# Multiply and GELU on one core: the last y load in shrinking pieces, the stores in growing ones

## Chip, core, metric

The kernel runs on one core of one Trainium2 chip. The metric is the device time of one execution in microseconds, as the median of several runs. All runs told of here were in the fast state, and the granted clock was 1.00 in each. The rounds of the experiments ran on different chips, so each run is compared with the kernel before in its own rounds.

## The reference

```python
x, y: float32, 1024 x 4096
z = x * y
out = 0.5 * z * (1 + tanh(sqrt(2 / pi) * (z + 0.044715 * z ** 3)))   # float32
```

16.8 MB are read for x, 16.8 MB for y, and 16.8 MB are written: 50.33 MB for two operations per element.

## The kernel before

Each tensor is viewed as 128 rows of 32768 columns, one row per SBUF partition (128 KB a row). x stays in SBUF whole and is overwritten in place; y passes through a ring of 16384 columns. All transfers are issued by SyncE (SP) into one queue. VectorE multiplies 4096 columns at a time, ScalarE applies GELU to them, and two stores of 16384 columns close the kernel.

```python
X_LOADS = [(0, 16384), (16384, 32768)]
Y_LOADS = [(0, 16384, 0), (16384, 24576, 0), (24576, 32768, 8192)]   # from, to, place in the ring
STEP = 4096
STORES = [(0, 16384), (16384, 32768)]
# ...
    _hoist(nc, [load_x(0).ins, load_y(0).ins])      # issued ahead of the start barrier
    load_x(1)
    for i in (1, 2):                                # a ring place is free after its multiplication
        nc.sync.wait_ge(sem_mul, (Y_LOADS[i][1] - Y_LOADS[1][0]) // STEP)
        load_y(i)
    n = 0
    for i, (a, b, r) in enumerate(Y_LOADS):
        # ... VectorE waits for x and y ...
        for c in range(a, b, STEP):
            nc.vector.tensor_mul(out=xs[:, c : c + STEP], in0=xs[:, c : c + STEP],
                in1=ys[:, r + c - a : r + c - a + STEP]).then_inc(sem_mul, 1)
            n += 1
            nc.scalar.wait_ge(sem_mul, n)
            nc.scalar.activation(out=xs[:, c : c + STEP], in_=xs[:, c : c + STEP],
                func=GELU).then_inc(sem_act, 1)
    for i, (a, b) in enumerate(STORES):
        nc.sync.wait_ge(sem_act, b // STEP)
        nc.sync.dma_start(out=out_r[:, a:b], in_=xs[:, a:b]).then_inc(sem_o[i], 16)
# ... wait for the stores, clear the semaphores ...
```

## Time and profile before

| | before |
|---|---|
| time, median of the 3 runs known at the prediction | 121.03 us (120.79 to 121.08) |
| span of the profiled run | 119.5 us |
| VectorE busy, ScalarE busy | 35.0 us, 30.2 us |
| share of the DMA queue's packets in 16 engines' span | 98.5% |
| last store issued; its first packets | 93.3 us; 99.3 us |

Some readings rest on the packet records of the trace, which lie under the profile's DMA rows. Each record is one packet of one engine with start, duration and size. A partition row is one packet here (896 data packets for 7 transfers of 128 rows), and after each transfer comes a packet of 4 bytes per engine (112 of them), followed by the 16 increments of its semaphore. I also use the times at which these 16 semaphore increments land, as the mean over the engines. In the rows of digits, the GB/s rows and the stretches below, a packet's time and bytes are counted whole where it starts.

### The profile page before, as it was taken

The page shows a single profiled execution, that of the slowest core. Times are in us where ns is not written, and L with a number is a line of the kernel's source. Part 1 is how long each engine was busy: PE and PEld are TensorE (multiplying, and loading weights), DVE is VectorE, ACT ScalarE, POOL GpSimd, SP SyncE. Part 2 cuts the span into 40 slices and gives each one's busy share as a digit, 9 for nine tenths or more (in the row PEclk, how much of TensorE's full clock was granted, in tenths as well). Part 3 has the DMA queues.
Part 4 walks back from the last instruction along what each step waited for, and adds up shares of the span by engine and source line. Part 5 has one row for each costly group of instructions (what it writes and reads, how often), then busy time and mean ns, then how long its engine had stood idle before and what let it go on. Part 6 is the DMA issues. An engine that isn't in the chain of part 4 may idle for free.

```text
span 119.5 us, 68 instructions
## 1 busy us (share of the span) xinstructions
DVE 35.0 (29%) x8; ACT 30.2 (25%) x9; POOL 0.2 (0%) x4
## 2 busy tenths in 40 slices
DVE  0000000000000199999600049959990000000000
ACT  3000000000000006797780000977479200000000
POOL 0000000000000000000000000000000000000000
DMA  9889888998899889988898989998899888988890
GB/s 351 351 373 680 351 351 351 636 417 351 351 636 417 351 351 526 526 351 351 351 526 351 504 373 482 395 526 351 351 395 658 351 351 351 702 351 351 351 680 22
DMA packets 1008, 50.33 MB, mean 421 GB/s; under 512 B 112, under 2 KB 112, under 8 KB 112
## 3 DMA queue, kind: packets, MB, share of 16 engines
q1 hardware_dynamic: 1008, 50.33, 98.5%
HBM read 33.55 MB, written 16.78 MB: 421 GB/s over the span
## 4 chain that ended last, share of the span: by engine, by line
DMA 53%; DVE 22%; ACT 3%; SPq 0%; issue 0%; DVEq 0%
DMA ys<-in_y_dram 53%; DVE xs L87 22%; ACT xs L94 3%; SPq L66 0%; DVEq L85 0%
## 5 line engine op out<-in xcount | busy, mean ns | idle before, releaser
L87 DVE TENSOR_TENSOR xs<-xs,ys 128x4096 f32<-128x4096 f32 x8 | 35.0, 4421 | 54.7 <-DMA ys<-in_y_dram 54.7
L94 ACT ACTIVATE xs<-xs 128x4096 f32<-128x4096 f32 x8 | 28.9, 3617 | 61.1 <-DVE xs L87 61.1
L94 ACT ACT_TABLE_LOAD x1 | 1.3, 1283 | 1.9 <-PEq L54 1.9
L120 POOL MEMSET const-bfloat16-1.0<- 128x1 bf16 x1 | 0.1, 102 | 0.0
L120 POOL MEMSET const-uint8-127<- 128x1 uint8 x1 | 0.1, 102 | 0.0
L120 POOL MEMSET const-float32-1.0<- 128x1 f32 x1 | 0.1, 99 | 0.0
L120 POOL MEMSET const-float32-0.0<- 128x1 f32 x1 | 0.1, 98 | 0.2 <-issue 0.2
## 6 DMA issues: line engine op xcount, KB each, us to landing
ys<-in_y_dram SPq DMA_DIRECT2D x2, 4096.0 KB, 21.1
xs<-in_x_dram SPq DMA_DIRECT2D x2, 40.3
out_dram<-xs SPq DMA_DIRECT2D x2, 31.9
ys<-in_y_dram SPq DMA_DIRECT2D x1, 40.8
```

The costliest lines, as they stand in the source:

```text
L87: nc.vector.tensor_mul(out=xs[:, c : c + STEP], in0=xs[:, c : c + STEP], in1=ys[:, r + c - a : r + c - a + STEP],).then_inc(sem_mul, 1)
L94: nc.scalar.activation(out=xs[:, c : c + STEP], in_=xs[:, c : c + STEP], func=GELU).then_inc(sem_act, 1)
L120: nc = _bacc.Bacc("TRN2", target_bir_lowering=False, num_devices=1)
```

## The change

The intent: load less and less towards the end, so that little computing remains after the last byte of y, and start the stores small.

```diff
-Y_LOADS = [(0, 16384, 0), (16384, 24576, 0), (24576, 32768, 8192)]
+Y_LOADS = [(0, 16384, 0), (16384, 24576, 0), (24576, 28672, 8192),
+    (28672, 30720, 12288), (30720, 31744, 14336), (31744, 32768, 15360)]
-STORES = [(0, 16384), (16384, 32768)]
+STORES = [(0, 1024), (1024, 2048), (2048, 4096), (4096, 8192), (8192, 16384), (16384, 32768)]
@@
-    for i in (1, 2):
-        nc.sync.wait_ge(sem_mul, (Y_LOADS[i][1] - Y_LOADS[1][0]) // STEP)
+    for i in range(1, len(Y_LOADS)):
+        nc.sync.wait_ge(sem_mul, -(-(Y_LOADS[i][1] - Y_LOADS[1][0]) // STEP))
@@  (the multiplication and the activation take w = min(STEP, b - c) columns)
+            done[c + w] = n
@@
-        nc.sync.wait_ge(sem_act, b // STEP)
+        nc.sync.wait_ge(sem_act, done[min(k for k in done if k >= b)])
```

More of the change, by code (lines that the diff above doesn't have):

```diff
@@ L13 @@
 X_LOADS = [(0, 16384), (16384, 32768)]
-Y_LOADS = [(0, 16384, 0), (16384, 24576, 0), (24576, 32768, 8192)]
-STEP = 4096
-STORES = [(0, 16384), (16384, 32768)]
+Y_LOADS = [
+    (0, 16384, 0),
+    (16384, 24576, 0),
+    (24576, 28672, 8192),
+    (28672, 30720, 12288),
+    (30720, 31744, 14336),
+    (31744, 32768, 15360),
+]
+STEP = 4096
+STORES = [
+    (0, 1024),
+    (1024, 2048),
+    (2048, 4096),
+    (4096, 8192),
+    (8192, 16384),
+    (16384, 32768),
+]
 Y_RING = 16384
@@ L75 @@
     load_x(1)
-    for i in (1, 2):
-        nc.sync.wait_ge(sem_mul, (Y_LOADS[i][1] - Y_LOADS[1][0]) // STEP)
+    for i in range(1, len(Y_LOADS)):
+        nc.sync.wait_ge(sem_mul, -(-(Y_LOADS[i][1] - Y_LOADS[1][0]) // STEP))
         load_y(i)
     n = 0
+    done = {}
     for i, (a, b, r) in enumerate(Y_LOADS):
@@ L86 @@
         for c in range(a, b, STEP):
+            w = min(STEP, b - c)
             nc.vector.tensor_mul(
-                out=xs[:, c : c + STEP],
-                in0=xs[:, c : c + STEP],
-                in1=ys[:, r + c - a : r + c - a + STEP],
+                out=xs[:, c : c + w],
+                in0=xs[:, c : c + w],
+                in1=ys[:, r + c - a : r + c - a + w],
             ).then_inc(sem_mul, 1)
             n += 1
+            done[c + w] = n
             nc.scalar.wait_ge(sem_mul, n)
             nc.scalar.activation(
-                out=xs[:, c : c + STEP], in_=xs[:, c : c + STEP], func=GELU
+                out=xs[:, c : c + w], in_=xs[:, c : c + w], func=GELU
             ).then_inc(sem_act, 1)
     for i, (a, b) in enumerate(STORES):
-        nc.sync.wait_ge(sem_act, b // STEP)
+        nc.sync.wait_ge(sem_act, done[min(k for k in done if k >= b)])
         nc.sync.dma_start(out=out_r[:, a:b], in_=xs[:, a:b]).then_inc(sem_o[i], 16)
```

## The prediction

The forecast came to 121.03 + 0.3 - 0.3 = 121.0 us. Both terms stand below.

Two numbers help. 16 packets of 64 KB in 2.414 us are 434 GB/s; read "the ceiling" in the fourth rival as that rate. And an estimate from the trace of the kernel before, made afterwards, gives about the times that part (4) goes on with: two multiplications of 4096 columns take 8.76 us there, so VectorE would end near 79.2 + 8.8 = 88.0 us; a quarter of an activation of 3.62 us, 0.9, makes it 88.9, some 4 us before 93.3.

> **What bounds the kernel now.** I began with the busy shares of the page, then its forty slices, then the chain that ended last, then the engines' busy time by stretch and the order of instructions in time, and last the single packet records that lie under the DMA rows.
>
> ```profile
> DVE 35.0 (29%) x8; ACT 30.2 (25%) x9; POOL 0.2 (0%) x4
> DMA  9889888998899889988898989998899888988890
> DMA packets 1008, 50.33 MB, mean 421 GB/s; under 512 B 112, under 2 KB 112, under 8 KB 112
> q1 hardware_dynamic: 1008, 50.33, 98.5%
> ```
>
> VectorE and ScalarE work less than a third of the span. The DMA queue is busy for 98.5% of 16 engines' span, in every slice but the last. So the bytes set the time. A chain of waits draws another picture, and a reader must not be taken in by it:
>
> ```profile
> 0.44 40.80 DMA ys<-in_y_dram
> 41.34 17.44 DVE xs L87 x4
> 58.80 21.99 DMA ys<-in_y_dram
> 80.88 8.77 DVE xs L87 x2
> 89.68 3.62 ACT xs L94
> ```
>
> This chain ends with the last activation at 93.3 us, and the span ends at 119.5. From it one would say that the last y load, its two multiplications and its activation delay the last store: 80.8 to 93.3 us, 12.5 us that smaller pieces could shorten. The order in time shows why that is not what ends the kernel:
>
> ```profile
> 50.13 9.00 SPq L70 DMA_DIRECT2D ys<-in_y_dram  x2
> 62.45 31.22 SPq L100 DMA_DIRECT2D out_dram<-xs  x2
> 79.26 3.62 ACT L94 ACTIVATE xs<-xs 128x4096 f32<-128x4096 f32 x1 [0.72 <-DVE xs L87]
> 80.88 8.76 DVE L87 TENSOR_TENSOR xs<-xs,ys 128x4096 f32<-128x4096 f32 x2 [1.66 <-DMA ys<-in_y_dram]
> 89.68 3.62 ACT L94 ACTIVATE xs<-xs 128x4096 f32<-128x4096 f32 x1 [0.72 <-DVE xs L87]
> ```
>
> The first store was issued at 62.45 us, while loads were still queued, and waits its turn. By the packet records it runs on each engine from about 80.0 to 99.3 us. The second store is issued at 93.32 us (62.45 + 31.22 less its own issue of 0.34), about 6 us before the engines come to it. The work in stretches agrees: the DMA share stays near 1 while VectorE computes, and the dip of the last row is the tail after the last packets.
>
> ```profile
> 0.00:59.90 59.90, 17.43 (x4) 13.23 (x5) 0.20 (x4) 1.00 0.99 421
> 59.90:79.90 20.00, 8.76 (x2) 6.78 (x3) 0.00 (x0) 1.00 1.00 418
> 79.90:119.50 39.60, 8.76 (x2) 10.21 (x3) 0.00 (x0) 1.00 0.98 424
> ```
>
> The packet records explain the span almost fully. Each engine carries 8 packets of each transfer (128 partition rows over 16 engines), one packet per row: 40 of 64 KB, 16 of 32 KB, and one of 4 bytes after each transfer. A 64 KB packet takes 2.418 us and overlaps the next by 0.004, so 2.414; a 32 KB one 1.213, so 1.209. Sum per engine: 40 x 2.414 + 16 x 1.209 + 7 x 0.006 = 96.6 + 19.3 + 0.04 = 115.9 us. Around it: 1.0 us to the first packet, 0.7 more for the first packet (2.6 to 3.3 us in place of 2.42), 0.35 from last data to the last semaphore, 0.1 to 0.5 by which engines differ. That leaves some 0.9 us of slow packets. (The time of the profiled run is 120.85 us, 1.35 over its span; I carry that difference over unchanged.) 0.15 of them are spread over 50 to 58 us. The other 0.7 sits in one place: on all 16 engines the last load packet but one takes 1.67 to 1.93 us instead of 1.213 (0.46 to 0.72 more), and the last one up to 0.22 more; the next packet is the first of the store. No load-to-load or store-to-store border shows such a loss. I call it the turn from loads to stores; it is the only idle capacity on the path that this change can reach.
>
> [...]
>
> **The change part by part.** (1) Bytes: the same 50.33 MB, so 115.9 us per engine stays, apart from the packet overhead. (2) Packets: loads of y go from 3 to 6, stores from 2 to 6, transfers from 7 to 14. Data packets per engine go from 56 to 112: 32 of 64 KB, and 16 each of 32, 16 and 8 KB, and 32 of 4 KB. Two 32 KB packets cost 2.418 against 2.414 for one of 64 KB, so about 0.0045 us per extra packet: 56 x 0.0045 = 0.25 us. Seven more semaphore packets at 0.006 add 0.04. Together +0.3. [...] I take +0.3[...].
>
> (3) Issue: seven more instructions of 0.33 us on SP, 2.3 us. The y pieces wait for multiplications 3, 4, 4, 4, i.e. for about 54.5 and 58.8 us; the last is out near 60, the four smaller stores by about 61.5, the 8192-column one after activation 4 at 62.4. The engines then still have the y load at 16384 in hand until about 69.6. Nothing runs dry; the 2.3 us lie beside the transfers.
>
> (4) Compute: the y load of 8192 columns lands at 70.4 as before and keeps VectorE until 79.2. The pieces of 4096, 2048, 1024 and 1024 (landing between about 75 and 80.8) then find VectorE busy, and go back to back[...]. The last store is issued some 4 us earlier than at 93.3. Its turn comes at 99.3 either way, so its lead grows from 6 to 10 us and the time gains nothing.
>
> (5) The turn: with 32 KB rows before and 64 KB rows after it, it costs 0.7 us. With 4 KB on both sides, the last two load packets last 0.3 us together. If the loss goes with the size of packets that are in hand together, it falls to about 0.1 us, a gain of 0.6. If it is a fixed latency, it stays. I give these about 55 to 45, a mean of -0.3.
>
> Sum: 121.03 + 0.3 - 0.3 = 121.0 us.
>
> **The rivals.** First, the gain that the chain of waits suggests: a shorter tail from last y to last store. It would be worth up to 4 us[...], so about 117. Against it speaks the first store, which fills the queue from 80 to 99.3; I give it next to nothing. Second, the turn gets cheap, and packets cost as computed: 120.7. For it speaks that exactly two packets before the first store are slow, on all 16 engines[...]. Third, the turn costs the same 0.7 and overhead comes on top: 121.3 to 121.6. The slow first packet of the kernel, about 0.7 us as well, speaks for a fixed latency. Fourth, 4 KB rows run far below the ceiling[...]: each of the four small transfers has 1.2 us of data, 4.8 in all, and at half the rate they would add 4.8 us and give 126. Nothing in this trace has rows so small[...]. Fifth, the queue cannot hold some ten transfers at once (three in the kernel before) and SP blocks. It would delay issues, not empty the engines, and the last store has 10 us to spare: no change.
>
> **Range and chances.** 121.0 us, between 120.4 (turn gone, little overhead, a good run) and 121.9[...]; the three runs before alone spread by 0.3. Two per cent are 2.4 us. For a gain of that size the queue would have to have been idle for as long, and it is not: 0.01. For a loss of that size the fourth rival must come true at half its strength: 0.04. Within: 0.95.
>
> **What would show it right or wrong.** The DMA queue's share stays at 98% or more, with the same bytes and 2,016 packets. The last store is issued near 89 us and its first packet still starts near 99 to 100. A 4 KB packet takes 0.15 to 0.17 us; at 0.3 the fourth rival has come true. The sum of extra time in the last load packets is 0.1 or 0.7 us and decides between the second and third rival. If any engine shows a gap between packets, or the last store is issued after its turn, the argument is wrong.

## The result

The changed kernel takes 121.16 us (121.04 to 121.58, 6 runs), the kernel before 120.95 us in its 6 runs. The ratio is 1.0024, with a 95% interval of 1.0006 to 1.0043. Such a ratio is the mean time of one kernel's fast runs over that of the other's fast runs of the same rounds, so it is not quite the ratio of the medians. By the rule of 2% the kernels are equal; by the interval the change costs between 0.1 and 0.5 us.

The page of the changed kernel: busy engines, the DMA row in forty slices, packets, and the queue's share.

```profile
DVE 35.0 (29%) x10; ACT 30.3 (25%) x11; POOL 0.2 (0%) x4
DMA  9899888988899889988999989999999999988990
DMA packets 2017, 50.33 MB, mean 420 GB/s; under 512 B 225, under 2 KB 225, under 8 KB 737
q1 hardware_dynamic: 2016, 50.33, 98.5%
```

The bytes and the queue's share are the same, and packets have doubled to the 2,016 foretold. The chain of waits (start, duration, what) and the order of instructions in time, of the same kernel:

```profile
58.74 18.91 DMA ys<-in_y_dram
79.04 4.43 DVE xs L103
83.49 7.31 ACT xs L111 x4
```

```profile
50.07 10.00 SPq L84 DMA_DIRECT2D ys<-in_y_dram  x5
60.12 31.03 SPq L117 DMA_DIRECT2D out_dram<-xs  x6
70.36 17.57 DVE L103 TENSOR_TENSOR xs<-xs,ys 128x4096 f32<-128x4096 f32 x6 [11.64 <-DMA ys<-in_y_dram]
83.49 7.31 ACT L111 ACTIVATE xs<-xs 128x4096 f32<-128x4096 f32 x4 [0.72 <-DVE xs L103]
```

The last activation ends at 83.49 + 7.31 = 90.80 us instead of 93.3, so the computing did become shorter, by 2.5 us. The span is 119.8 us instead of 119.5. VectorE no longer waits for the last pieces at all: six multiplications follow each other from 70.36 us.

The packet records show the rest. A 64 KB packet takes 2.418 us as before, one of 16 KB 0.611, of 8 KB 0.309, of 4 KB 0.159, each overlapping the next by about 0.004. No engine is dry for more than 0.3 us anywhere. (One sign of being wrong, "any engine shows a gap", thus came true by the letter: at 78.3 to 78.7 us, inside the turn, some engine stands for up to 0.23 us at a stretch. In the kernel before no such gap reaches 0.06 us there.) The last store's first packets start at 99.3 to 100.0 us, against 99.3 to 99.7 before, though it was issued at 90.8.

The turn from loads to stores can be seen in the work by stretch (columns: stretch, its length, VectorE, ScalarE and GpSimd busy with the number of instructions, granted clock, DMA share, GB/s). Because a packet's bytes count where it starts, in a short stretch of large packets the rate jumps about, and only that of a stretch of small ones can be taken at its word. First the kernel before, then the changed one, each with a quiet stretch of the y load at column 16384 above the stretch before the first store:

```profile
67.00:69.60 2.60, 0.00 (x0) 0.00 (x0) 0.00 (x0) 1.00 0.99 429
76.70:79.30 2.60, 2.53 (x1) 1.88 (x2) 0.00 (x0) 1.00 1.20 403
```

```profile
67.00:69.60 2.60, 0.00 (x0) 0.00 (x0) 0.00 (x0) 1.00 0.99 429
76.70:79.30 2.60, 2.60 (x2) 1.88 (x2) 0.00 (x0) 1.00 0.97 321
```

The 403 of the kernel before still hangs on where its few packets start; the 321 of the changed kernel, whose packets are small there, is a real dip against 429. The changed kernel's rate alone from 76 to 82 us, in forty slices of 0.15 us:

```profile
GB/s 273 601 273 601 246 492 273 355 382 410 328 355 273 300 246 218 219 164 355 355 355 355 410 437 410 437 410 410 410 437 382 437 410 410 437 410 437 437 437 410
```

Between 77.8 and 78.7 us the rate falls to about half, while the engines are still loading y; the first store packet starts at 79.8 us or later. So the turn is still there. I measure it from the mean landing of the y load at column 16384 to that of the last y piece, less the packets' usual time: 8 x 1.209 + 0.006 = 9.68 us for one piece of 8192 columns; for the four pieces 8 x 0.607, 8 x 0.306 and 16 x 0.1553 us, plus 4 x 0.006, 9.81 us in all. The kernel before took 10.37 us, the changed one 10.38. So the turn cost 0.69 us before and 0.56 after, in one profile each. Read from the 4-byte packets instead of the landings, the same turns are 0.71 and 0.56; over all runs the two readings differ by up to 0.1 us, so a difference of 0.1 between two turns says nothing.

### The profile page after: what moved, and what is told of

Read it like the earlier page. It is cut to its first block, busy times and chain, and to the rows that moved or that the text cites. A ratio compares the mean times of both kernels' runs of the same rounds, so it can differ in the third digit from the quotient of the medians.

```text
span 119.8 us, 84 instructions
## 1 busy us (share of the span) xinstructions
DVE 35.0 (29%) x10; ACT 30.3 (25%) x11; POOL 0.2 (0%) x4
## 3 DMA queue, kind: packets, MB, share of 16 engines
q1 hardware_dynamic: 2016, 50.33, 98.5%
## 4 chain that ended last, share of the span: by engine, by line
DMA 50%; DVE 18%; ACT 6%; issue 1%; SPq 0%; DVEq 0%
DMA ys<-in_y_dram 50%; DVE xs L103 18%; ACT xs L111 6%; SPq L80 0%; DVEq L100 0%
## 5 line engine op out<-in xcount | busy, mean ns | idle before, releaser
L103 DVE TENSOR_TENSOR xs<-xs,ys 128x4096 f32<-128x4096 f32 (+2 forms) x10 | 35.0, 3565 | 52.9 <-DMA ys<-in_y_dram 52.9
L111 ACT ACTIVATE xs<-xs 128x4096 f32<-128x4096 f32 (+2 forms) x10 | 29.0, 2928 | 58.6 <-DVE xs L103 58.6
```

The lines of the kernel that those rows point to most:

```text
L103: nc.vector.tensor_mul(out=xs[:, c : c + w], in0=xs[:, c : c + w], in1=ys[:, r + c - a : r + c - a + w],).then_inc(sem_mul, 1)
L111: nc.scalar.activation(out=xs[:, c : c + w], in_=xs[:, c : c + w], func=GELU).then_inc(sem_act, 1)
```

## The experiments

All outputs are right. Turns are measured as above, or in the same way at the place where a run has moved them, from the one profile of each run.

### 1. Only the y pieces

```diff
 # from the changed kernel
+STORES = [(0, 16384), (16384, 32768)]
```

> Only the y pieces of the change, the stores as before. Packets: 24 more per engine at 0.0045 us and 3 more transfers at 0.006, so +0.13 us. Theory 'small loads': the turn from loads to stores is cheaper because the last load packets are small (0.5 instead of 0.7 us, as in the changed kernel), so the sum is about -0.05 us against the kernel before. Theory 'small stores': the first store's packet size sets the turn; here it is 64 KB, so the turn stays 0.7 and the time rises by 0.13. Theory 'fixed': like the second.

Measured: 121.09 us against 120.98 for the kernel before, ratio 1.0012 (0.9995 to 1.0028). The turn cost 0.83 us, more than in either kernel so far. Its stretch of the profile shows the deepest dip of the runs with small loads:

```profile
76.70:79.30 2.60, 2.60 (x2) 1.88 (x2) 0.00 (x0) 1.00 0.98 279
```

The theory "small loads" expected 0.5 us there and failed in this run. The interval of the time spans 0.4 us and cannot separate -0.05 from +0.13.

### 2. Only the growing stores

```diff
 # from the changed kernel
+Y_LOADS = [(0, 16384, 0), (16384, 24576, 0), (24576, 32768, 8192)]
```

> Only the growing stores of the change, the last y load as before. 32 more packets and 4 more transfers: +0.17 us. Theory 'small loads': the turn stays 0.7 us in the last two load packets, +0.17 against the kernel before. Theory 'small stores': the turn falls to about 0.5, so about 0.0. Theory 'fixed': 0.7, +0.17.

Measured: 121.17 us, ratio 1.0012 (0.9998 to 1.0026). The turn cost 1.16 us, the most of all runs, though the first stores are of 4 KB rows. That speaks against "small stores": the size of the first store does not make the turn cheap.

### 3. Two turns

```diff
 # from the kernel before
-STORES = [(0, 16384), (16384, 32768)]
+STORES = [(0, 8192), (8192, 16384), (16384, 24576), (24576, 32768)]
 # SP issues: y at 16384, store 0, y at 24576, stores 1 to 3
```

> Stores of 8192 columns; the first goes between the last two y loads, so the queue turns from loads to stores twice (at about 69.5 and 89 us), and once back. 16 more packets, 2 more transfers: +0.08. Theory 'turn': the slow load packets appear before each of the two turns, at about 67 to 69 and 86 to 88 us, 0.7 us each, and none at 77 to 79 us: +0.8 in all, more if the way back costs too. Theory 'moment' (the loss belongs to the moment near 78 us, to what VectorE and ScalarE do then, or to those rows of y): the loss stays single, +0.1.

Measured: 121.34 us, ratio 1.0031 (1.0015 to 1.0047), so about +0.4 us. At the first turn, near 69 us, the y load at 16384 landed 10.65 us after x instead of 9.72 in the kernel before: 0.93 us lost, all of it again in the last two load packets of each engine. At the second turn, near 89 us, the load packets ran clean; from the one y landing to the other it took 19.44 us for 2 x 9.68, so 0.08 us. At 77 to 79 us there was no slow packet. So the loss does not belong to the moment or to what VectorE does then; it moved with the turn. But it came once, not twice. Neither theory had that. From here on I asked what sets a first store apart.

### 4. All tail pieces and all stores of 1024 columns

```diff
 # from the changed kernel: the last 8192 columns of y in 8 loads, the stores in 32
+STORES = [(1024 * k, 1024 * k + 1024) for k in range(32)]
```

> The last 8192 columns of y in 8 loads and all stores in 32, each of 1024 columns: 352 data packets per engine instead of 56, 44 transfers instead of 7. With the 0.0045 us per packet and 0.006 per transfer of the traces: 296 x 0.0045 + 37 x 0.006 = +1.55, less 0.2 for the turn: about +1.3 us. [...] If the queue of SP cannot keep up with 0.45 us per issue against 1.24 us of data per transfer: gaps between packets, and more than that.

Measured: 122.03 us, ratio 1.0088 (1.0073 to 1.0103), so +1.06 us against some +1.3 expected. The packets account for it within 0.2 us: by size and count they sum to 117.43 us per engine instead of 115.94, +1.49; what the last y loads lost beyond their packets was 0.44 us instead of 0.69. The stores of 512 KB (4 KB rows), queued back to back, landed every 1.245 us on average, which is 421 GB/s, 3% less than the 434 of 64 KB packets. SP kept up, though it stood in one issue for 5.3 us. Of the 0.44 us (0.34 by the 4-byte packets) half or more fell at 70 to 71 us, where the 4 KB loads begin, far ahead of the first store; I do not know why. By the 4-byte packets the last two loads ahead of the first store lost only 0.07 us together.

### 5. Delays in the computing

```diff
 # kernel before, or the changed one; ahead of the multiplications of the last y piece
+            for d in range(3):     # or 10
+                nc.vector.wait_ge(sem_d, d + 1)
+                nc.vector.tensor_mul(out=dummy, in0=dummy, in1=dummy).then_inc(sem_d, 1)
```

The tile is a scratch of 128 x 1024. The kernel before with 3:

> The kernel before with 3 extra multiplications of 1024 columns on VectorE (about 1.27 us each, one waiting for the other) ahead of the last two real ones: the last activation and the last store's issue move from 93.3 to about 97.1 us. Theory 'queue' (the last store has 6 us of lead until its turn at 99.3): no change, within 0.2 us. Theory 'chain' (the chain of waits to the last activation sets the end): +3.8 us.

Measured: 120.78 us, ratio 0.9987 (0.9970 to 1.0004). The order in time shows the store issued 3.83 us later than in the kernel before:

```profile
81.06 3.74 DVE L92 TENSOR_TENSOR idle_work<-idle_work 128x1024 f32<-128x1024 f32 x3 [1.95 <-issue]
97.15 0.34 SPq L107 DMA_DIRECT2D out_dram<-xs  x1
```

Nothing was lost (120.93 us for the kernel before in the same rounds). The chain of waits had named exactly these multiplications, and a delay of 3.83 us in them cost nothing. The kernel before with 10:

> As before with 10 extra multiplications, about 12.5 us: the last store is issued near 105.8 us. Theory 'queue': the engines run dry from about 99.6 us until 1 us after the issue, so +7 us. Theory 'chain': +12.5 us.

Measured: 127.96 us, so +7.0 us, as "queue" had it (ratio 1.0583, 1.0568 to 1.0599). The DMA row, in slices of 3.2 us, shows the hole between the first store and the second, two slices in which no packet starts:

```profile
DMA  9797797799799779779899799797797007799777
```

The changed kernel with 10:

> The changed kernel with the same 10 extra multiplications ahead of its last piece of 1024 columns: VectorE ends near 100.4 instead of 87.9 us, the last activation of 1.06 us near 101.5. Theory 'queue': engines dry from about 99.6 to 102.6, so +3 us against the changed kernel, some 4 us less than the same delay costs the kernel before. Theory 'chain': +10.7 us or more (90.8 to 101.5).

Measured: 123.75 us against 120.93 for the kernel before (ratio 1.0243, 1.0219 to 1.0267). Against the changed kernel's 121.16, measured in other rounds, that is +2.6; +3 was expected. The last activation took 1.06 us, from 100.47. With the same delay the changed kernel is 4.2 us faster than the kernel before (127.96 less 123.75). This is what the change buys: a lead for the last store, worth nothing until something uses it up.

### 6. A small store first

```diff
 # from the kernel before
+STORES = [(0, 1024), (1024, 16384), (16384, 32768)]
 # SP issues store 0 after activation 1, ahead of the y load at 16384
```

> The kernel before, with the first 1024 columns of the first store issued right after activation 1 (near 49.5 us), ahead of the y load at 16384, so that a small store (512 KB) passes the engines near 60 us; the rest of the stores as before. In the two-turn run only the first turn was slow. Theory 'first store': the loss (0.7 to 1.2 us so far) moves to the load packets just before 60 us and there is none at 77 to 79 us; time within 0.2 us of before. Theory 'every turn': about 0.8 us at both places, time +0.8. Theory 'size': a turn to only 1.2 us of store costs little, and the loss at 77 to 79 us stays: +0.1 to +0.2.

Measured: 121.03 us, ratio 1.0005 (0.9992 to 1.0018). The last two load packets of x ahead of the small store, at 57 to 60 us, lost 0.69 us (x landed 20.04 us after y instead of 19.35). The large turn at 80 us lost nothing: from one y landing to the other 9.71 us. "First store" was right, "every turn" and "size" wrong. A store of 512 KB, about 1.2 us of data, took the whole loss here, and the large one behind more loads lost 0.03 us (9.71 less 9.68).

### 7. Two attempts to take the first store out of the way

```diff
 # a: kernel before; first of all transfers, on SP, waited for ahead of the last store
+    nc.sync.dma_start(out=out_r[:, total_f - 128 :], in_=x_r[:, total_f - 128 :])
 # b: kernel before; on ScalarE's queue after a memset of the tile, waited for likewise
+    nc.scalar.dma_start(out=out_r[:, total_f - 128 :], in_=zero)
```

> The kernel before, with a small copy from x to the last 128 columns of the output (64 KB, HBM to HBM) issued ahead of all loads; the real last store waits for it and writes over it. It costs about 0.2 to 1 us at the start. Theory 'first write to HBM' (the engines pay once when they first write to HBM, whatever the source): the loss at 77 to 79 us is gone, and the time is from -0.7 to +0.3. Theory 'first read of SBUF' or 'turn': the loss stays, time +0.2 to +1.

Measured: 121.83 us, ratio 1.0076 (1.0059 to 1.0092). The loss stayed: 10.64 us between the y landings, 0.97 lost. The small copy itself delayed the start: the first x packets started at 1.9 us instead of 1.0.

> The kernel before, with a small store of 128 zero columns from SBUF (64 KB) issued by ScalarE's queue near 2 us into the columns that the last store writes over after waiting for it. It passes the engines beside the first x packets, on another ring. Theory 'first store': the loss at 77 to 79 us is gone; if the early one hides in the slow start, the time falls by up to 0.7 us, if it is paid there, no change. Theory 'first store of this queue' or 'turn': the loss stays at 77 to 79 us, time +0.1 to +0.3.

Measured: 121.06 us, ratio 1.0011 (0.9997 to 1.0024). The early store's packets came between 6.3 and 24 us, among those of x and y, and not near 2 us. The loss stayed: 0.79 us. So neither a first write to HBM in SP's queue nor a first store from SBUF in another queue takes the loss away. Only an earlier store from SBUF in SP's own queue did (runs 3 and 6).

### 8. The stores in another queue

```diff
 # from run 1; both stores on ScalarE's queue
+            if n == 5:
+                nc.scalar.wait_ge(sem_y[4], 16)
+                store(0, 4)        # nc.scalar.dma_start after sem_act >= 4
```

> The y pieces of the change, two stores, but both stores are issued by ScalarE's queue, the first only when the last y piece but one has landed (near 79 us), so it is not queued behind the loads. Its first packet comes about 1 us after the issue, some 0 to 0.7 us after the last load data. If the loss at 77 to 79 us comes from the store waiting in the same queue, the load packets there run clean (0.155 us each) and y lands 0.7 us earlier; what is left is the dry moment, and possibly a slow first store packet. Theory 'first store': about 0.7 us are lost at or just before the first store packets all the same, time +0.1 to +0.9 with the dry moment. Theory 'queue': nothing is lost but the dry moment, time -0.6 to +0.2.

Measured: 120.62 us against 120.81 for the kernel before, ratio 0.9983 (0.9970 to 0.9997). The first store was issued at 79.01 us. The load packets ran clean: the y landings were 9.92 us apart, 0.11 us over the packets' time (0.01 by the 4-byte packets). The stretch that dipped to 279 and 321 GB/s holds its rate:

```profile
76.70:79.30 2.60, 2.60 (x2) 1.78 (x1) 0.00 (x0) 1.00 1.00 407
```

Its rate from 76 to 82 us in slices of 0.15 us shows no dip at 78 us, and then the dry moment ahead of the first store's large packets. They count whole where they start, near 80 us, so the zeros after them are no pause:

```profile
GB/s 492 382 437 437 437 328 355 382 437 382 437 410 437 410 437 437 410 437 410 437 437 355 219 82 27 1311 5680 0 0 0 0 0 0 0 0 0 0 0 0 0
```

The first store packets themselves were not slow (2.46 us instead of 2.42). The engines are dry for about 0.4 us (mean end of the last load packets to mean start of the first store packets). And the engines end closer together: their last increments land within 0.20 us, against 0.45 in the kernel before and 0.77 in the changed one. Most of the gain lies there and not in the turn: the mean landing of the last store came only 0.05 us earlier than in the kernel before (119.08 instead of 119.12), the last of its 16 increments 0.22 us earlier. What the clean loads saved, the dry moment took back for the most part.

> The same with a store of 64 KB by ScalarE's queue near 2 us, as in the run with the early store from SBUF, whose packets showed no loss at the start. Theory 'first store of a queue': the loss was hidden in the slow start and is absent near 79 us; 0.5 to 0.9 us faster than the run without the early store, about -0.6 against the kernel before. Theory 'turn of the queue from loads to stores', or any in which the ScalarE queue does not matter: the same as the run without the early store, within 0.2 us.

Measured: 120.70 us, ratio 0.9989 (0.9977 to 1.0002), the same as without the early store. So "first store of a queue, hidden by an early one" fell, and so did "first store" as such: here the first store of all did not make the load packets slow (407 GB/s over 76.7 to 79.3 us without the early store, 406 with it). What was right is the reading "queue": in these runs the loss comes when the first store stands in the loads' queue behind loads. These two runs change the queue and the moment of issue together; which of the two does it, I cannot tell from them.

Run 8 without the early store is the fastest, 0.2% below the kernel before in the same rounds. Its ratio of 0.9983 and the changed kernel's of 1.0024 are from different rounds, so their distance of 0.4% is only a comparison through the kernel before.

### What the turns say together

Queued behind loads of 32 KB rows, or of 64 KB rows in run 6, the first store cost 0.69 (before), 1.16, 0.93, 0.92, 0.96, 0.69, 0.97 and 0.79 us (runs 2, 3, 5 with 3, 5 with 10, 6, 7a, 7b): 0.89 on average. Behind the shrinking loads it cost 0.56 (changed), 0.83 (run 1) and 0.74 us (run 5): 0.71 on average. The ranges overlap. If shrinking loads help, then by about 0.2 us, and eleven single profiles do not prove it. Run 4, with all its tail loads of 4 KB rows, lost least of the kernels with a queued first store, 0.44 us, and little of it near the turn. Whether many small loads take the turn away or only move the loss, no run decides.

## Why the prediction was right, point by point

- **What bounds the kernel.** Right, and shown by runs 5: with 6 us of lead, 3.8 us of delay cost nothing, and 12.6 us cost 7.0.
- **Packets, +0.3 us.** Right: by the records 116.21 us per engine instead of 115.94, +0.27. Run 4 with 5 times the extra packets (296 data packets per engine and 37 transfers, +1.49 us) confirms the rate.
- **Issue.** The five y loads were out at 60.1 us and nothing ran dry outside the turn, as said. The fifth rival came true without harm: SP stood in the issue of the 8192-column store for 6.6 us, with one transfer running and eight waiting, each of 9 packets per engine.
- **Compute.** VectorE ended at 87.93 us, against 88.0 in the estimate beside the prediction. The end of the activations was mis-sized: 90.80 us instead of near 89. I added one activation after VectorE's end, but ScalarE started the piece of 4096 columns only at 83.49 us and needs 7.31 us for the four. The last store's lead is thus 8.5 us and not 10. It moved no time. The last activation itself took 1.04 us, more than a quarter of 3.62: the activations here took 1,038, 1,892 and 3,617 ns for 1024, 2048 and 4096 columns. The multiplications took 1,216, 2,282 and 4,420 ns.
- **The turn, -0.3 us on average between 0 and -0.6.** This is the term that was mis-sized. It measured 0.13 us less in the profiled pair, about 0.2 over all profiles. And the reading behind the larger gain, that two packets are affected whatever their size, was wrong: with 4 KB packets, 55 packets (3 to 4 per engine on average) took over 0.03 us more than 0.159, between 77.0 and 79.5 us, while in the kernel before the two slow ones lie between 76.8 and 80 us. The -0.3 was the mean of two outcomes, a gain of 0.6 and none; neither came true, and what was measured lies nearer to none.
- **Sum.** 0.27 - 0.13 = +0.14 us expected from the measured terms; the mean landing of the last store came 0.10 us later in the profiled pair, 119.23 instead of 119.12. The span grew by 0.3, because the slowest engine ended 0.49 us after the mean instead of 0.29. This spread was in no step of the prediction. It first grows in the small load pieces (0.50 us at the second of them, 0.99 at the third), where the turn hits the engines unevenly. Run 1 had only 0.42 at its end with the same pieces, so it is not certain to come with the change. That 121.0 came within 0.2 us of 121.16 is therefore in part luck: the turn gave less than half of what was forecast. That the time would hardly move was no luck, because the queue left nothing larger to gain.
- **Rivals.** The shorter tail (117 us) and slow 4 KB rows (126 us) are both refuted. So is the cheap turn (120.7 us): it needed a loss near 0.1 us. The third rival, a turn that costs the same with the overhead on top (121.3 to 121.6), lies as near to what was measured as the sum of 121.0 does.

What makes the loss at the first queued store stays open. Shown is: except in run 4, it falls on load packets in the last 2 to 3 us ahead of the store's first packet; it came once where two turns were made (0.93 and 0.08 us in run 3, 0.69 and 0.03 in run 6); it moved with the first store from SBUF in the loads' queue (to 69 us in run 3, to 60 us in run 6); and it was all but absent when that store was issued late and from the other queue (0.11 us in run 8).

## What to carry to other kernels

A chain of waits that ends well before the span ends (93.3 of 119.5 us here) need not be what sets the end; look at what stood in the queue in the meantime, and test it with a delay put into the chain (3.83 us cost nothing here). With the DMA queue full from start to end (98.5%), the smaller pieces ended the computing 2.5 us sooner and only bought lead, and cost about 0.0045 us per extra packet on each engine. Where the last tenths count, look at the load packets ahead of the first store, and try the stores from a second queue, issued when the last load is about to end (0.2% here).
